# A Strassen-form matmul kernel: shared homes for mixer tiles, a seventh pair of weight tiles in Strassen's form, and another order of the weight chunks

## The chip, the cores and the metric

The kernel runs on one core of a Trainium2 chip. The metric is the device time of one execution in microseconds (us). A core has five engines with queues of their own: TensorE (PE; PEld is its weight load), VectorE (DVE), ScalarE (ACT), GpSimd (POOL) and SyncE (SP, which here only issues transfers). Each engine works through its queue in order; an instruction that waits holds all behind it.

## What is computed

One layer of a decoder for 256 positions and a width of 4096, in float32. The normalised input `u` is multiplied by `w_in` (4096 x 28672). Its columns feed two mixers, a gated linear recurrence (HGRN2, 16 heads of 128) and differential attention (8 heads of 256), and two sigmoid gates. The mixers' outputs are projected, gated, added, projected by `w_out`, added to the input and normalised. Nearly all arithmetic is matmul against weights that are read once:

```python
u = rmsnorm(h, norm_w[l])
proj = u @ w_in[l]
...
y = (jax.nn.sigmoid(gate_a) * (o_a @ w_branch_a[l])
     + jax.nn.sigmoid(gate_b) * (o_b @ w_branch_b[l]))
h = h + y @ w_out[l]
```

Each head's mixer output goes through an RMS norm of its own (segments of 128 columns for HGRN2, 256 for attention) and is multiplied by the SiLU of a gate.

## The kernel before

**Numbers in two parts.** Each float32 operand is split into a rounded part `hi` and the rest `lo`; a product is three matmuls (hi hi, hi lo, lo hi). ScalarE copies a weight chunk into `hi` (line 162), VectorE subtracts to get `lo` (line 163). A chunk is 128 partitions by 1024 columns, or 512. Rings of 5 buffers each (`whi`, `wlo`) hold the split chunks; after the mixers two more of each are added. Weights arrive in a ring of three raw tiles `w` (128 x 2048, 1 MB), loaded by SyncE's queue.

**Units and pairs.** The program is a list of units, each a product of 256 rows with 1024 columns: 16 mixer units (numbered 0 to 15; two per group of heads, four HGRN groups, then four attention groups), 8 gate units (0 to 7), 8 half-length branch units and 4 output units. A unit runs over 16 pairs of 128-row weight tiles (a pair is one raw tile). A plain pair is 2 chunks, 4 output blocks each: 2 x 4 x 3 = 24 matmuls of 512 columns. A pair in Strassen's form ("S", in Winograd's variant) has 7 products, 21 matmuls, for which VectorE first makes sums of the weight blocks in the raw tile; it gives four chunks, the third of them of 512 columns. The sums of the other operand (`sf`, by `s_form`) are made once and kept in the pool `sp`, so the number of pairs in S form is limited by SBUF. Which pairs are in S form is a table of positions: `SPLIT` for mixer units 3 to 15 and gate units 0 and 1, `SPLIT_G` for gate units 2 to 6. Mixer units 0 to 2 and gate unit 7 are plain.

**The order of the work.** `Stream.take` splits weight chunks ahead of the matmuls: with `ahead` 3 in the mixers and gate unit 0 and 5 later. `ORDER` says which of the seven products each of the four chunks feeds; `p5`, `P1`, `P6`, `P7` have PSUM banks of their own, 0 to 3 are the output blocks. A scheduler places each engine's instructions; splits and the evictions at a unit's end have a higher priority than the rest. The sums of an S pair stand in `sums`: the first at chunk 0 (line 143), with it the 512-column difference `wt` in a pool of its own (line 144), and at chunk 2 the wide difference (line 148). The third chunk is split from `wt`.

**Mixer steps.** What a mixer does beside the big product (transposes, scan, scores, values, norm, gate) are small steps in a first-in, first-out list. After each pair `step(n)` takes the next two, or one if it uses TensorE, and those with TensorE only after pairs 14, 15, 0, 1 and 2, since their PSUM banks are those of the S products. Their tiles are `big` ones (128 x 1024, 4 KB per partition) with one home per name: `z`, `q`, `g`, `v`, `s1`, `s2`, and beside these `sc` (one and a half big tiles), `kx` and `qx` (half of one each). A new tile under a name waits for the last reader of the one before. `finish` makes the squares' sums by a reduction (line 697) over squares that ScalarE wrote (lines 862 and 963), and applies norm and gate in two wide multiplies (lines 710 and 711).

## Time and profile before

| | |
|---|---|
| median of 3 runs | 2788.42 us (2786.64 to 2789.74) |
| the profiled execution | 2788.72 us, its span 2786.9 us |
| TensorE, matmuls busy | 2760.9 us, 99% |
| TensorE, weight loads busy | 2274.4 us, 82% |
| VectorE busy | 2341.9 us, 84% |
| ScalarE busy | 1616.8 us, 58% |
| transfers | 597.76 MB, 214 GB/s over the span |
| weight load of 1 MB, issue to landing | 4.8 us (median) |

Rows of a group read: line, engine, operation, out<-in, shape, count, then the busy time, the mean length of one in ns, and the idle time of the engine just ahead of them with what ended it. Rows of a timeline read: start in us, length, engine, line, operation, and in brackets the engine's idle time ahead of it and what ended that. Rows of windows read: the stretch, its length, and each engine's busy time in it.

### The profile page before, as it was taken

To read this page: it belongs to the slowest core of one execution; us is meant where nothing else is said; L and a number is where in the kernel's file an instruction comes from. 1 tells how busy PE (TensorE), PEld (TensorE's weight loads), DVE (VectorE), ACT (ScalarE), POOL (GpSimd) and SP (SyncE) were. 2 spreads that over 40 slices of the span, in tenths; PEclk is the share of its full clock that TensorE was granted. 3 is DMA by queue.
4 is the path that set the end of the run, shared out by engine and by line. 5 is a ranking of instruction groups with operands and counts; after the bars stand their busy time and mean duration, and the time that the engine had idled before them with its cause. 6 is when DMAs were issued, how large, how long until landed. Compare 5 with 4: busy or idle time off the path is not lost.

```text
span 2786.9 us, 32847 instructions
## 1 busy us (share of the span) xinstructions
PE 2760.9 (99%) x12361; PEld 2274.4 (82%) x12361; DVE 2341.9 (84%) x2689; ACT 1616.8 (58%) x1937; POOL 74.6 (3%) x124
## 2 busy tenths in 40 slices
PE   9999999999999999999999999999999999999998
PEld 7888888888888888888888887778888888888886
DVE  6784888888888888888888899999877878989997
ACT  7664656656555555665556555555655554555554
POOL 0010000000000000000000000000000000010000
PEclk9999999999999999999999999999999999999999
DMA  9555455555555555555556555555675766766665
GB/s 343 188 181 203 180 185 202 198 199 193 188 191 210 190 192 187 198 206 189 191 196 245 201 212 211 222 214 201 241 263 218 250 218 227 259 235 237 248 255 214
DMA packets 96767, 597.76 MB, mean 214 GB/s; under 512 B 11856, under 2 KB 12128, under 8 KB 31200
## 3 DMA queue, kind: packets, MB, share of 16 engines
q1 hardware_dynamic: 88272, 566.29, 55.9%
q0 software_dynamic: 8336, 29.38, 2.8%
q8 instruction: 96, 1.57, 0.2%
q14 instruction: 63, 0.52, 0.1%
HBM read 571.51 MB, written 24.12 MB: 214 GB/s over the span
## 4 chain that ended last, share of the span: by engine, by line
PE 78%; DVE 14%; DMA 4%; issue 2%; ACT 2%; POOL 0%; DVEq 0%; ACTq 0%; POOLq 0%
PE ps_w L286 75%; DVE lo L163 9%; DVE w L148 2%; DMA w<-in_w_gate 1%; ACT hi L162 1%; DMA w<-in_w_out 1%; DVE w L143 1%; DVE wt L144 1%; PE ps_q L759 1%; DMA w<-in_w_mix 0%; DMA yl<-y_dram 0%; DVE ut L369 0%; PE ps_sc L842 0%; PE ps_o L857 0%; PE ps_t L718 0%
## 5 line engine op out<-in xcount | busy, mean ns | idle before, releaser
L162 ACT ACTIVATE hi<-w 128x1024 fp32r<-128x1024 f32 (+1 forms) x1203 | 1231.5, 1053 | 1009.8 <-PE ps_w L286 497.4
L163 DVE TENSOR_TENSOR lo<-w,hi 128x1024 fp32r<-128x1024 f32 (+1 forms) x1203 | 1436.9, 1219 | 309.0 <-ACT hi L162 291.8
L286 PE MATMUL ps_w<-hi,u 128*128 128x512 f32 x4794 | 1538.8, 391 | 2.0 <-ACT hi L162 2.0
L286 PEld LDWEIGHTS ps_w<-hi,u 128*128 128x128 f32 x4794 | 900.6, 188 | 189.9 <-ACT hi L162 3.4
L286 PE MATMUL ps_w<-lo,u 128*128 128x512 f32 x2397 | 935.5, 390 | 0.9 <-DVE lo L163 0.9
L286 PEld LDWEIGHTS ps_w<-lo,u 128*128 128x128 f32 x2397 | 450.5, 188 | 99.0 <-DVE lo L163 7.1
L286 PE MATMUL ps_w<-hi,sf 128*128 128x512 f32 x1400 | 490.0, 390 | 0.8 <-ACT hi L162 0.7
L286 PEld LDWEIGHTS ps_w<-hi,sf 128*128 128x128 f32 x1400 | 262.8, 188 | 56.9 <-ACT hi L162 1.6
L286 PE MATMUL ps_w<-lo,sf 128*128 128x512 f32 x700 | 274.1, 392 | 8.1 <-DVE lo L163 7.9
L286 PE MATMUL ps_w<-hi,oh 128*128 128x512 f32 x864 | 272.4, 390 | 0.0
L286 PE MATMUL ps_w<-hi,y 128*128 128x512 f32 x784 | 250.1, 390 | 0.0
L148 DVE TENSOR_TENSOR w<-w,wt 128x1024 f32<-128x1024 f32 x175 | 213.6, 1220 | 0.3
L286 PEld LDWEIGHTS ps_w<-hi,oh 128*128 128x128 f32 x864 | 162.2, 188 | 34.3 <-DVE ut L531 1.0
L286 PEld LDWEIGHTS ps_w<-hi,y 128*128 128x128 f32 x784 | 147.2, 188 | 30.7 <-DVE ut L623 0.3
L286 PE MATMUL ps_w<-lo,oh 128*128 128x512 f32 x432 | 168.4, 390 | 0.0
L286 PEld LDWEIGHTS ps_w<-lo,sf 128*128 128x128 f32 x700 | 131.3, 188 | 41.5 <-DVE lo L163 14.7
L143 DVE TENSOR_TENSOR w<-w 128x512 f32<-128x512 f32 x175 | 120.5, 690 | 48.5 <-DMA w<-in_w_mix 27.0
L286 PE MATMUL ps_w<-lo,y 128*128 128x512 f32 x392 | 152.6, 389 | 0.0
L162 ACT ACTIVATE hi<-wt 128x512 fp32r<-128x512 f32 x175 | 109.8, 628 | 48.0 <-PE ps_w L286 32.1
L144 DVE TENSOR_TENSOR wt<-w 128x512 f32<-128x512 f32 x175 | 120.6, 689 | 2.8
L163 DVE TENSOR_TENSOR lo<-wt,hi 128x512 fp32r<-128x512 f32 x175 | 120.1, 686 | 1.8 <-ACT hi L162 1.8
L286 PEld LDWEIGHTS ps_w<-lo,oh 128*128 128x128 f32 x432 | 81.1, 188 | 16.6
(206 smaller groups left out, 1106.5 us busy)
## 6 DMA issues: line engine op xcount, KB each, us to landing
w<-in_w_mix SPq DMA_DIRECT2D x252, 1024.0 KB, 4.8
w<-in_w_gate SPq DMA_DIRECT2D x128, 1024.0 KB, 4.8
w<-in_w_branch SPq DMA_DIRECT2D x64, 1024.0 KB, 4.8
w<-in_w_out SPq DMA_DIRECT2D x64, 1024.0 KB, 5.3
gl<-g_dram SPq DMA_DIRECT2D x32, 256.0 KB, 3.7
g_dram<-ut POOLq DMA_DIRECT2D x28, 256.0 KB, 5.4
o_dram<-s POOLq DMA_DIRECT2D x8, 512.0 KB, 5.9
ol<-o_dram SPq DMA_DIRECT2D x16, 256.0 KB, 4.2
```

The source lines that it names most:

```text
L143: dve.tensor_tensor(w[:, 0:512], w[:, 0:512], w[:, 512:1024], op=ALU.add)
L144: dve.tensor_tensor(t, w[:, 0:512], w[:, 1536:2048], op=ALU.subtract)
L148: dve.tensor_tensor(b, b, t.unsqueeze(1).to_broadcast([P, 2, 512]), op=ALU.subtract)
L162: act.activation(hi[:, k : k + m], t[:, k : k + m], AF.Copy)
L163: dve.tensor_tensor(lo[:, k : k + m], t[:, k : k + m], f32(hi[:, k : k + m]), op=ALU.subtract)
L286: pe.matmul(ps[b], a, w, start=first, stop=left[b] == 0)
L759: pe.transpose(ps[:, j], r[:, j * P : (j + 1) * P], ident)
```

## The change

Five things change together.

1. **Homes.** `sc`, `kx`, `qx` and `wt` lose their own memory. Scores go into `s1` and into the first half of the old `b` tile (home `s2`), whose two halves take `kx` and `qx`; attention's exponentials take `s1` and `s2`, its transposed weights `q`; the mixer's output moves from `s2` to `z`, the gate's SiLU from `z` to `s2`.
2. **Norm.** ScalarE's squares are taken per segment with a running sum (`accum_out`), ahead of the copy, so the squares' tile and VectorE's reduction go. Norm and gate are applied in one instruction per segment, 8 of 128 columns for HGRN2 or 4 of 256 for attention, in place of two of 1024.
3. **A seventh pair.** `sp` holds 7 tiles, not 6. `SPLIT` is (4, 6, 7, 9, 10, 12, 13), was (4, 6, 8, 10, 12, 13). `SPLIT_G` keeps nine positions, with 0 and 8 out and 7 and 9 in: (2, 4, 6, 7, 9, 10, 12, 13, 14).
4. **Chunk order of an S pair.** The raw columns 1024 to 2047 (output blocks 0 and 1) come first, `p5` and `P1` second. The narrow difference is written in place over columns 1536 to 2047 once the first chunk has been split, and the wide difference follows it.
5. **`SPLIT_AHEAD`** is 4, was 3.

```diff
--- before.py
+++ after.py
@@ -35,7 +35,7 @@
 HALF = PIECE // 2
-SPLIT_AHEAD = 3
+SPLIT_AHEAD = 4
 HEAD = 4
@@ -50,8 +50,7 @@
     wlo = ctx.enter_context(tc.tile_pool(name="wlo", bufs=5))
-    wt = ctx.enter_context(tc.tile_pool(name="wt", bufs=1))
-    sp = ctx.enter_context(tc.tile_pool(name="sp", bufs=6))
+    sp = ctx.enter_context(tc.tile_pool(name="sp", bufs=7))
     gp = ctx.enter_context(tc.tile_pool(name="gp", bufs=5))
         def __init__(self):
@@ -136,16 +136,12 @@
 
-        def sums(self, i, c):
+        def sums(self, i):
             w = self.raw[i]
-            if c == 0:
-                t = self.raw[i, "T"] = wt.tile([P, 512], F32, name="wt", tag="wt")
-                dve.tensor_tensor(w[:, 0:512], w[:, 0:512], w[:, 512:1024], op=ALU.add)
-                dve.tensor_tensor(t, w[:, 0:512], w[:, 1536:2048], op=ALU.subtract)
-            if c == 2:
-                t = self.raw[i, "T"]
-                b = w[:, 512:1536].rearrange("p (a c) -> p a c", a=2)
-                dve.tensor_tensor(b, b, t.unsqueeze(1).to_broadcast([P, 2, 512]), op=ALU.subtract)
+            t2 = w[:, 1536:2048]
+            dve.tensor_tensor(t2, w[:, 0:512], t2, op=ALU.subtract)
+            b = w[:, 512:1536].rearrange("p (a c) -> p a c", a=2)
+            dve.tensor_tensor(b, b, t2.unsqueeze(1).to_broadcast([P, 2, 512]), op=ALU.subtract)
 
@@ -153,9 +149,15 @@
                 with tc.high_priority(AHEAD):
+                    o = c * HALF
                     if self.kind[i] == "S":
-                        self.sums(i, c)
-                    t = self.raw[i, "T"] if c == 2 else self.raw[i][:, (0, 1024, 0, 512)[c] :]
+                        if c == 0:
+                            w = self.raw[i]
+                            dve.tensor_tensor(w[:, 0:512], w[:, 0:512], w[:, 512:1024], op=ALU.add)
+                        if c == 2:
+                            self.sums(i)
+                        o = (1024, 0, 1536, 512)[c]
+                    t = self.raw[i][:, o:]
                     w = 512 if c == 2 else HALF
@@ -163,7 +165,6 @@
                     del self.raw[i]
-                    self.raw.pop((i, "T"), None)
                 self.split[self.done] = (hi, lo)
@@ -260,7 +261,7 @@
 
-    ORDER = (("p5", "P1"), (0, 1), ("P6",), ("P7", 2))
+    ORDER = ((0, 1), ("p5", "P1"), ("P6",), ("P7", 2))
 
@@ -435,10 +436,10 @@
 
-    SPLIT = (4, 6, 8, 10, 12, 13)
-    SPLIT_G = (0, 2, 4, 6, 8, 10, 12, 13, 14)
+    SPLIT = (4, 6, 7, 9, 10, 12, 13)
+    SPLIT_G = (2, 4, 6, 7, 9, 10, 12, 13, 14)
     us = {}
-    s_pools = [sp] * 6
+    s_pools = [sp]
 
@@ -460,7 +461,7 @@
         if n == 0:
-            s_pools[:] = [sp2] * 3
+            s_pools[:] = [sp2]
         if n in SPLIT_G and n not in SPLIT:
@@ -569,7 +570,7 @@
                 if n == 0:
-                    s_pools[:] = [sp] * 6 + [sp2]
+                    s_pools[:] = [sp]
                     s_pool.at = -1
@@ -681,34 +682,29 @@
 
-        def half(tag):
-            return tmp.tile([P, HPG, P], F32, name=tag, tag=tag)
-
         def rows(t):
...
             n = 1024 // seg
-            o, sq, g = T["o"], T["sq"], T["g"]
+            o, ss, g = T["o"], T["ss"], T["g"]
 
             def stats():
-                ss = tmp.tile([P, n], F32, name="ss", tag="ss", bufs=2)
-                dve.tensor_reduce(ss, fl(sq).rearrange("p (n c) -> p n c", c=seg), axis=AX.X, op=ALU.add)
                 act.activation(ss, ss, AF.Sqrt, scale=1.0 / seg, bias=eps)
                 dve.reciprocal(ss, ss)
-                T["ss"] = ss
 
             def gate():
-                sg = big("z")
+                sg = big("s2")
                 act.activation(fl(sg), fl(g), AF.Sigmoid)
...
             def apply():
-                o3 = fl(o).rearrange("p (n c) -> p n c", c=seg)
-                dve.tensor_tensor(o3, o3, T["ss"].unsqueeze(2).to_broadcast([P, n, seg]), op=ALU.mult)
-                dve.tensor_tensor(fl(o), fl(o), fl(T["silu"]), op=ALU.mult)
+                for i in range(n):
+                    c = slice(i * seg, (i + 1) * seg)
+                    dve.scalar_tensor_tensor(fl(o)[:, c], fl(o)[:, c], ss[:, i : i + 1], fl(T["silu"])[:, c],
+                                             op0=ALU.mult, op1=ALU.mult)
 
@@ -819,24 +815,24 @@
             def s1d():
-                km, kx, dec = T["z"], half("kx"), T["dec"]
-                dve.tensor_tensor(km, km, T["sg"], op=ALU.mult)
-                dve.tensor_tensor(kx, km[:, :, 0:P], dec[:, :, 1].to_broadcast([P, HPG, P]), op=ALU.mult)
-                T["kx"] = kx
+                dve.tensor_tensor(T["z"], T["z"], T["sg"], op=ALU.mult)
 
             def s2():
-                qm, qx, dec = T["q"], half("qx"), T["dec"]
+                qm, km, dec = T["q"], T["z"], T["dec"]
                 dve.tensor_tensor(qm, qm, T["b"], op=ALU.mult)
-                dve.tensor_tensor(qx, qm[:, :, P:S], dec[:, :, 2].to_broadcast([P, HPG, P]), op=ALU.mult)
-                T["qx"] = qx
+                x = fl(T["b"]).rearrange("p (x h c) -> p x h c", x=2, h=HPG)
+                dve.tensor_tensor(x[:, 0], km[:, :, 0:P], dec[:, :, 1].to_broadcast([P, HPG, P]), op=ALU.mult)
+                dve.tensor_tensor(x[:, 1], qm[:, :, P:S], dec[:, :, 2].to_broadcast([P, HPG, P]), op=ALU.mult)
+                T["x"] = x
 
...
                     if tb == 0:
-                        T["sc"] = tmp.tile([P, 3, HPG, P], F32, name="sc", tag="sc")
-                    sc = T["sc"][:, tb]
+                        s = fl(big("s1")).rearrange("p (t h c) -> p t h c", t=2, h=HPG)
+                        T["sc"] = s[:, 0], s[:, 1], T["x"][:, 0]
+                    sc = T["sc"][tb]
                     c = slice(tb * P, (tb + 1) * P)
-                    k, q = (T["kx"], T["qx"]) if tb == 2 else (T["z"][:, :, c], T["q"][:, :, c])
+                    k, q = (T["x"][:, 0], T["x"][:, 1]) if tb == 2 else (T["z"][:, :, c], T["q"][:, :, c])
                     ps = spare([P, HPG, P], "ps_sc")
@@ -849,17 +845,21 @@
                     if tb == 0:
-                        T["o"], T["sq"] = big("s2"), big("s1")
+                        T["o"] = big("z")
+                        T["ss"] = tmp.tile([P, 1024 // P], F32, name="ss", tag="ss", bufs=2)
                     sc, v = T["sc"], rows(T["v"])
...
                         c = slice(h * P, (h + 1) * P)
-                        pe.matmul(ps[:, h], sc[:, tb, h], v[:, tb, c], start=True, stop=(tb == 0))
+                        pe.matmul(ps[:, h], sc[tb][:, h], v[:, tb, c], start=True, stop=(tb == 0))
                         if tb:
-                            pe.matmul(ps[:, h], sc[:, 2, h], v[:, 0, c], start=False, stop=True)
+                            pe.matmul(ps[:, h], sc[2][:, h], v[:, 0, c], start=False, stop=True)
                     pf = ps.rearrange("p h c -> p (h c)")
-                    act.activation(rows(T["o"])[:, tb], pf, AF.Copy)
-                    act.activation(rows(T["sq"])[:, tb], pf, AF.Square)
+                    o = rows(T["o"])[:, tb]
+                    for h in range(HPG):
+                        i = tb * HPG + h
+                        act.activation(o[:, h * P : (h + 1) * P], ps[:, h], AF.Square, accum_out=T["ss"][:, i : i + 1])
+                    act.activation(o, pf, AF.Copy)
                 return f
@@ -910,11 +910,9 @@
                                        channel_multiplier=1, compare_op=ALU.is_ge, fill=NEG)
-                    if hh == 0:
-                        T["ee"] = tmp.tile([P, 3, HPG, P], F32, name="ee", tag="sc")
-                    ee = T["ee"].rearrange("p a h c -> p (a h c)")[:, 768 * hh : 768 * (hh + 1)]
+                    ee = fl(big(("s1", "s2")[hh]))
                     e0 = ee[:, :256].rearrange("p (i s) -> p i s", i=2)
-                    e1 = ee[:, 256:].rearrange("p (i s) -> p i s", i=2)
+                    e1 = ee[:, 256:768].rearrange("p (i s) -> p i s", i=2)
                     for qb, e in ((0, e0), (1, e1)):
@@ -944,23 +942,29 @@
                     pe.transpose(ps[:, S : S + P], e1[:, 0, P:S], ident)
-                    aT = half(("kx", "qx")[hh]).rearrange("p h c -> p (h c)")
-                    act.activation(aT[:, : 3 * P], ps[:, : 3 * P], AF.Copy)
+                    if hh == 0:
+                        T["aq"] = fl(big("q"))
+                    aT = T["aq"][:, hh * 384 : (hh + 1) * 384]
+                    act.activation(aT, ps[:, : 3 * P], AF.Copy)
                     T["aT", hh] = aT
...
                     if hh == 0:
-                        T["o"], T["sq"] = big("s2"), big("s1")
+                        T["o"] = big("z")
+                        T["ss"] = tmp.tile([P, 1024 // 256], F32, name="ss", tag="ss", bufs=2)
                     aT, v = T["aT", hh], rows(T["v"])
...
                     pe.matmul(ps[:, 1], aT[:, S : S + P], v[:, 1, c], start=False, stop=True)
-                    act.activation(rows(T["o"])[:, :, c], ps, AF.Copy)
-                    act.activation(rows(T["sq"])[:, :, c], ps, AF.Square)
+                    o = rows(T["o"])[:, :, c]
+                    for t in range(2):
+                        i = 2 * t + hh
+                        act.activation(o[:, t], ps[:, t], AF.Square, accum_out=T["ss"][:, i : i + 1])
+                    act.activation(o, ps, AF.Copy)
                 return f
```

How instructions move on VectorE. In the names `w` is the raw tile, `hi` and `lo` the split chunk. Before the change, in mixer unit 7, around the neighbouring S pairs 12 and 13 (L143 is an S pair's first sum, L144 its `wt`, L148 its wide difference); the piece begins with the wide difference of pair 12:

```order
L148 TENSOR_TENSOR w<-w,wt 128x1024
L143 TENSOR_TENSOR w<-w 128x512
L144 TENSOR_TENSOR wt<-w 128x512
L163 TENSOR_TENSOR lo<-w,hi 128x1024 x3
L163 TENSOR_TENSOR lo<-wt,hi 128x512
L148 TENSOR_TENSOR w<-w,wt 128x1024
L163 TENSOR_TENSOR lo<-w,hi 128x1024
L315 TENSOR_TENSOR ut<-ps_w,ut 128x512
```

Both narrow sums of pair 13 stand ahead of the last `lo` of pair 12, and between the wide difference of pair 13 and its last `lo` stands nothing.

With the change, in mixer unit 11, pairs 7 to 10 (L156 is an S pair's first sum, L142 the narrow difference in place, L144 the wide one, L165 `lo`); the piece begins with the narrow difference of pair 7:

```order
L142 TENSOR_TENSOR w<-w 128x512
L165 TENSOR_TENSOR lo<-w,hi 128x1024
L165 TENSOR_TENSOR lo<-w,hi 128x512
L144 TENSOR_TENSOR w<-w 128x1024
L156 TENSOR_TENSOR w<-w 128x512
L165 TENSOR_TENSOR lo<-w,hi 128x1024 x5
L142 TENSOR_TENSOR w<-w 128x512
L156 TENSOR_TENSOR w<-w 128x512
L144 TENSOR_TENSOR w<-w 128x1024
L165 TENSOR_TENSOR lo<-w,hi 128x512
L165 TENSOR_TENSOR lo<-w,hi 128x1024 x3
L142 TENSOR_TENSOR w<-w 128x512
```

The narrow difference of pair 7 has moved behind the `lo` of that pair's first chunk, the one of pair 9 (behind the run of five `lo`) behind its second; the narrow `lo` of the third chunk has moved next to the wide difference, in pair 9 behind it.

The same queue and unit, from the third chunk of pair 10 to the end of pair 13:

```order
L165 TENSOR_TENSOR lo<-w,hi 128x512
L156 TENSOR_TENSOR w<-w 128x512
L165 TENSOR_TENSOR lo<-w,hi 128x1024 x5
L142 TENSOR_TENSOR w<-w 128x512
L156 TENSOR_TENSOR w<-w 128x512
L144 TENSOR_TENSOR w<-w 128x1024
L165 TENSOR_TENSOR lo<-w,hi 128x512
L165 TENSOR_TENSOR lo<-w,hi 128x1024 x3
L142 TENSOR_TENSOR w<-w 128x512
L144 TENSOR_TENSOR w<-w 128x1024
L165 TENSOR_TENSOR lo<-w,hi 128x512
L165 TENSOR_TENSOR lo<-w,hi 128x1024 x2
```

At pair 10 the first sum of pair 12 stands ahead of the last `lo`, the first entry of the run of five; at pairs 12 and 13 nothing stands between the narrow `lo` and the last.

On TensorE, with the change, in mixer unit 5 at the end of pair 10 (hi_4108 and lo_4109 are its last chunk, hi_4118 the first chunk of the plain pair 11; ps_w_3900 is the bank of `P7`):

```order
L287 MATMUL ps_w_3891<-hi_4094,sf_2082 128x512
L287 MATMUL ps_w_3891<-lo_4095,sf_2082 128x512
L287 MATMUL ps_w_3891<-hi_4094,sf_2082 128x512
L287 MATMUL ps_w_3900<-hi_4108,sf_2082 128x512
L287 MATMUL ps_w_3704<-hi_4108,u_115 128x512
L287 MATMUL ps_w_3692<-hi_4118,u_115 128x512
L287 MATMUL ps_w_3696<-hi_4118,u_115 128x512
L287 MATMUL ps_w_3700<-hi_4118,u_115 128x512
L287 MATMUL ps_w_3900<-lo_4109,sf_2082 128x512
L287 MATMUL ps_w_3900<-hi_4108,sf_2082 128x512
L287 MATMUL ps_w_3704<-lo_4109,u_115 128x512
```

Of the last chunk of pair 10 the products with `hi` and three of pair 11's have moved ahead of the first that reads lo_4109. At the end of pair 13 it is the same with two of pair 14's.

The program has 45 matmuls of 512 columns fewer than before (11718, were 11763).

## Prediction

> **What bounds the kernel now.** I read the page first: busy shares, the chain that ended last and the costliest group.
>
> ```profile
> span 2786.9 us, 32847 instructions
> PE 2760.9 (99%) x12361; PEld 2274.4 (82%) x12361; DVE 2341.9 (84%) x2689; ACT 1616.8 (58%) x1937; POOL 74.6 (3%) x124
> ...
> PE 78%; DVE 14%; DMA 4%; issue 2%; ACT 2%; POOL 0%; DVEq 0%; ACTq 0%; POOLq 0%
> ...
> L286 PE MATMUL ps_w<-hi,u 128*128 128x512 f32 x4794 | 1538.8, 391 | 2.0 <-ACT hi L162 2.0
> ```
>
> TensorE is the bound, but VectorE stands on the last chain for 14% of the span, so there are places where TensorE is fed late. A matmul's own 391 ns is no price, since matmuls overlap. The price comes from stages, so I cut the trace by windows at the first matmul of a unit: mixer units 6 and 10, then gate units 1 to 6.
>
> ```profile
> core 0: us, PE busy (x) PEld busy (x) DVE busy (x) ACT busy (x) POOL busy (x), PEclk, DMA share, GB/s
> 542.80:629.60 86.80, 86.80 (x400) 72.00 (x399) 72.34 (x75) 50.54 (x57) 0.55 (x1) 1.00 0.54 196
> 894.60:979.70 85.10, 85.10 (x385) 70.37 (x383) 71.43 (x74) 49.47 (x58) 0.55 (x1) 1.00 0.55 197
> ...
> 1505.80:1588.80 83.00, 83.00 (x368) 68.71 (x367) 74.21 (x86) 47.73 (x54) 1.79 (x4) 1.00 0.60 226
> 1588.80:1670.60 81.80, 81.46 (x358) 66.83 (x357) 75.27 (x84) 47.38 (x55) 1.61 (x3) 1.00 0.59 218
> 1670.60:1755.20 84.60, 82.67 (x359) 66.57 (x358) 79.33 (x86) 48.61 (x56) 2.16 (x4) 1.00 0.56 211
> 1755.20:1838.50 83.30, 82.07 (x358) 66.53 (x357) 77.91 (x85) 50.35 (x58) 2.16 (x4) 1.00 0.57 214
> 1838.50:1923.40 84.90, 82.51 (x359) 66.53 (x358) 80.23 (x87) 47.85 (x55) 2.16 (x4) 1.00 0.57 212
> 1923.40:2006.40 83.00, 82.07 (x358) 66.43 (x357) 78.00 (x85) 51.01 (x58) 2.17 (x4) 1.00 0.57 214
> ```
>
> Gate unit 1 holds 6 S pairs of 21 matmuls and 10 plain ones of 24, so 366 (the row's 368 counts neighbours that overlap its ends), with no gap: 83.00 / 366 = 0.2268 us per matmul at full clock. So a plain pair takes TensorE 5.44 us, an S pair 4.76. Gate units 2 to 6 hold 9 S pairs, 357 matmuls, 80.95 us; their five rows add up to 417.6, so 12.9 us are lost there. Mixer units lose nothing that counts: 86.80 is 366 matmuls (83.0) and the mixer's own small ones. VectorE is idle 14 us of each mixer unit but only 4.7 to 6.5 of a 9-S gate unit.
>
> **The change, part by part.**
>
> *The seventh pair.* Mixer units 3 to 15 and gate units 0 and 1 turn one plain pair into S form: 15 x 3 = 45 matmuls fewer, 45 x 0.2268 = **10.2 us off TensorE**. That is 0.68 us per unit.
>
> *What VectorE pays for it.* These rows are the forms that a pair is made of.
>
> ```profile
> L163 DVE TENSOR_TENSOR lo<-w,hi 128x1024 fp32r<-128x1024 f32 x1195 | 1431.8, 1223 | 308.6 <-ACT hi L162 291.4
> L162 ACT ACTIVATE hi<-w 128x1024 fp32r<-128x1024 f32 x1195 | 1226.9, 1056 | 1008.8 <-PE ps_w L286 497.4 <-DVE w L148 341.5 <-DVE w L143 68.2
> ...
> L148 DVE TENSOR_TENSOR w<-w,wt 128x1024 f32<-128x1024 f32 x175 | 213.6, 1220 | 0.3
> ```
>
> What a row costs in a full queue is the distance of starts, and the timeline of VectorE shows it, here for mixer unit 6 while it prepares the two neighbouring S pairs 12 and 13; behind it stand TensorE's first matmul on pair 12 and its first use of the last `lo` of pair 13, and ScalarE's `hi` for that chunk.
>
> ```profile
> 604.06 1.22 DVE L148 TENSOR_TENSOR w<-w,wt 128x1024 f32<-128x1024 f32 x1
> 605.20 0.69 DVE L143 TENSOR_TENSOR w<-w 128x512 f32<-128x512 f32 x1
> 605.92 0.69 DVE L144 TENSOR_TENSOR wt<-w 128x512 f32<-128x512 f32 x1
> 606.52 1.22 DVE L163 TENSOR_TENSOR lo<-w,hi 128x1024 fp32r<-128x1024 f32 x1
> 608.66 2.60 DVE L163 TENSOR_TENSOR lo<-w,hi 128x1024 fp32r<-128x1024 f32 x2 [0.91 <-ACT hi L162]
> 611.17 0.69 DVE L163 TENSOR_TENSOR lo<-wt,hi 128x512 fp32r<-128x512 f32 x1
> 611.77 1.22 DVE L148 TENSOR_TENSOR w<-w,wt 128x1024 f32<-128x1024 f32 x1
> 614.20 1.23 DVE L163 TENSOR_TENSOR lo<-w,hi 128x1024 fp32r<-128x1024 f32 x1 [1.21 <-ACT hi L162]
> ```
>
> ```profile
> 607.32 0.39 PE L286 MATMUL ps_w<-hi,sf 128*128 128x512 f32 x1
> ...
> 615.70 0.39 PE L286 MATMUL ps_w<-lo,sf 128*128 128x512 f32 x1
> ```
>
> ```profile
> 613.11 1.06 ACT L162 ACTIVATE hi<-w 128x1024 fp32r<-128x1024 f32 x1 [2.19 <-DVE w L148]
> ```
>
> Starts stand 1.14 us apart behind a 1024-wide row (604.06 to 605.20), 0.60 behind a 512-wide one (605.92 to 606.52), 0.72 where the next reads the result (605.20 to 605.92). An S pair is four wide rows and three narrow: 4 x 1.14 + 2 x 0.60 + 0.72 = 6.48 us of VectorE, a plain one 2.28. So a unit's VectorE gains 4.2 us of work while TensorE loses 0.68.
>
> On the average this fits: 72.34 + 4.2 = 76.5 of 86.1 us. But the seven pairs no longer alternate. Positions 7 to 13 run S P S S P S S, and the group P S S costs VectorE 2.28 + 2 x 6.48 = 15.24 us against 5.44 + 2 x 4.76 = 14.96 on TensorE: **VectorE has no spare time there, and each wait of its own is TensorE's.** Five `hi`/`lo` buffers let it stand four chunks ahead, no more.
>
> How near that is shows in the rows above: the last `lo` of pair 13 ended at 614.20 + 1.23 = 615.43, TensorE read it at 615.70, a margin of 0.27 us, with a plain pair between S pairs up to there.
>
> *The chunk order.* Raw columns 1024 to 2047 go first now, which need no sum. The narrow sum that feeds the third chunk (`wt`, now in place) can no longer be made ahead: it writes over columns that the first chunk reads, so it stands behind that chunk's `lo` at pair 7 and behind the second chunk's at pairs 9 to 13 (the first two listings of the change). In the old order it lay in front, at 605.92, in time that VectorE lost to ScalarE anyway (the 0.91 us ahead of 608.66). Now up to 0.72 us enter the chain to the last `lo`, less the 0.24 us that VectorE idles inside the two-row entry (2.60 against 1.14 + 1.22): about 0.5 net. Margin 0.27 - 0.5: TensorE waits about **0.25 us at pair 7**, the first neighbour pair.
>
> From there VectorE leads. Between the wide sum's start and the last `lo` lie 614.20 - 611.77 = 2.43 us (sum, ScalarE's `hi` from 613.11, signals). The sum fills 1.14, the narrow `lo`, now behind it, 0.60; the remaining 0.69 stays empty unless the next pair's first sum stands there, which the order gives for pair 10 alone (0.09). A group P S S so takes 15.24 + 0.09 + 0.69 = 16.0 us, 1.05 more than TensorE. Two groups, up to pairs 10 and 13: 2.1. With the 0.25: 2.35 us late at the last `lo` of pair 13.
>
> TensorE does not lose all of it. Its order there (last listing of the change) puts matmuls that need only `hi`, some of the next pair's, ahead of the first that needs this `lo`: at pair 10 four more than in a plain chunk, 4 x 0.2268 = 0.9 us; at pair 13 three, 0.7. With the larger the loss is 2.35 - 0.9 = **1.45 us per unit**. Ends: nothing lost, if VectorE enters pair 6 with more lead than at 615.43; 2.35, if the early matmuls hide nothing. I take 1.45, as both its parts come from rows of the same neighbourhood. Fourteen units (mixers 3 to 15, gate 0) have five buffers: +20.3 us. Gate unit 1 has seven and idles 83.00 - 74.21 = 8.8 us on VectorE: no loss.
>
> *Gate units 2 to 6* keep nine S pairs. Position 0 moves to 7: the unit boundary with its eight narrow eviction rows is relieved of 6.48 - 2.28 = 4.2 us, while 6 to 14 now hold seven S pairs in nine. Who is late there is known:
>
> ```profile
> PEld ps_w L286 <- DVE lo L163: 12.9, 17, 1.3
> ```
>
> that is, TensorE's weight loads, from 1588 us to 2094, for VectorE's `lo`. The unit's work on VectorE is unchanged, so what can shrink is its idle time of about 5 us: six uncovered waits of 0.69 and three of 0.09 make 4.4. Saved per unit: between 0 and 1 us; I take 0.4, **-2 us** in all, ends 0 and -5.
>
> *Mixer steps.* Nearest rows to what goes and comes:
>
> ```profile
> L932 ACT ACTIVATE ee<-ee,nm 128x128 f32<-128x128 f32 x16 | 6.3, 394 | 1.4 <-DVE nm L930 1.4
> ...
> L932 ACT ACTIVATION_READ_ACCUMULATOR ee<-ee,nm 128x1 f32 x32 | 6.0, 187 | 0.0
> ...
> L697 DVE TENSOR_REDUCE ss<-s 128x4 f32<-128x1024 f32 x4 | 4.9, 1220 | 2.9 <-ACT s L963 2.9
> ...
> L927 DVE SCALAR_TENSOR_TENSOR ee<-ps_s,bias 128x128 f32<-128x128 f32 x16 | 4.1, 282 | 3.8 <-PE ps_s L923 3.7
> ```
>
> Per HGRN group VectorE loses the reduction (1.22) and turns two wide multiplies (2 x 1.22, as the wide rows above) into eight of 128 columns (8 x 0.282 = 2.26); ScalarE's two squares become eight, each with an accumulator read: 8 x (0.394 + 0.187) = 4.6 us. All this stands beside plain pairs 15 and 0 to 3, where VectorE and ScalarE fill only 2.3 of 5.4 us per pair: nothing on the path. Uncovered, the 4.6 us on ScalarE would count in full: four groups, 18 us.
>
> [...]
>
> *Sum.* -10.2 + 20.3 - 2 = **+8.1 us** on the profiled execution's 2788.72 (span 2786.9 and 1.8 around it): 2796.8. The runs' median, 2788.42, is 0.3 lower: **2796.5 us**, 0.29% slower. Ends of the sum: -15 (2773) and +22.7 (2811).
>
> **The rivals.**
>
> *VectorE keeps its lead; faster.* The mixer's P S S groups lose nothing, because the waits for ScalarE lie where VectorE would wait for a buffer: -10.2 - 2, 2776. For it: idle 14 us per unit, a margin so far never below zero. Against: 15.24 over 14.96 leaves no place for any wait. It decides as soon as the loss per unit stays under 0.68 us.
>
> *A wash.* Early matmuls hide 1.6 us instead of 0.9; loss 0.75 per unit, 10.5 us, against 12.2: 2787.
>
> *VectorE as the bound throughout.* If its 14 us of idle time were all waits that stay, each added 4.2 us would count: 14 x 4.2 - 10.2 = +49, 2837. Against it: mixer units show TensorE without gaps. [...]
>
> *Shared homes block.* A tile that waits for its home holds ScalarE's or VectorE's queue, and the `hi` behind it: the 18 us above beside the forecast, 2815. Against: each home's last reader ran at least one pair earlier in the step list.
>
> **How the numbers follow.** Forecast 0.60, VectorE keeps its lead 0.14, a wash 0.21, the two others 0.05 together. What is under 0.2%, 5.6 us, can't be told from no change here: 2782.8 to 2794.0. Slower gets the forecast, less a little of its lower end, and the last two: 0.63; same the wash and that end: 0.23; faster: 0.14. The range runs from 2783, below the wash, to 2807, past the middle between the forecast and the sum's upper end.
>
> **What would show it.** Right: mixer units longer by about 0.8 us in spite of three matmuls fewer, with waits of weight loads or matmuls for `lo` at pairs 7, 10 and 13, where there were none; VectorE's idle before the last `lo` near 0.7; gate units 2 to 6 close to 83 us with their waits moved off the unit's first pairs. Wrong: mixer units 0.7 us shorter without such waits, or gate units near 81. A wait of ScalarE on a mixer tile would speak for blocked homes.

## The result

| | before | changed |
|---|---|---|
| median | 2787.79 us (4 runs, 2786.64 to 2789.74) | 2806.41 us (4 runs, 2804.05 to 2812.46) |
| the profiled execution, its span | 2788.72, 2786.9 | 2804.05, 2802.3 |

The changed kernel is slower: ratio 1.0069, interval 1.0057 to 1.0081, or +18.6 us between the medians. The forecast was 2796.5, +0.29%: the right side, but less than half of the loss. The two profiled executions lie 15.3 us apart, because that of the change is the fastest of its four (2.4 under its median) and that of before lies 0.9 above its median. What follows accounts for these 15.3.

The head of the page and the chain that ended last, changed kernel:

```profile
span 2802.3 us, 32888 instructions
PE 2766.6 (99%) x12316; PEld 2262.2 (81%) x12316; DVE 2382.6 (85%) x2788; ACT 1640.2 (59%) x2047; POOL 78.7 (3%) x124
...
PE 71%; DVE 16%; DMA 6%; ACT 4%; issue 2%; POOL 0%; ACTq 0%; DVEq 0%; POOLq 0%
```

45 matmuls fewer (12361 to 12316), and yet a longer span; TensorE's share of the last chain went from 78 to 71%. VectorE has 41 us more work, and its busy share went from 84 to 85%, which doesn't say where the time went. The windows by stage do. Before, mixer units 0 to 2, unit 1 of them, and units 3 to 15:

```profile
6.90:280.40 273.50, 273.01 (x1235) 226.67 (x1236) 187.61 (x250) 166.55 (x222) 8.44 (x4) 0.99 0.62 228
97.60:189.80 92.20, 91.93 (x428) 76.64 (x426) 84.79 (x123) 61.15 (x80) 7.06 (x2) 1.00 0.50 183
280.40:1421.50 1141.10, 1140.82 (x5192) 943.53 (x5191) 966.80 (x1091) 687.69 (x828) 13.39 (x19) 1.00 0.54 195
```

Changed: units 0 to 2, unit 1 of them, units 3 to 15, of these 6 and 10; then gate units 0 and 1, and gate units 2 to 6 together.

```profile
6.60:285.20 278.60, 273.80 (x1236) 227.62 (x1237) 187.59 (x261) 168.22 (x237) 12.57 (x4) 0.99 0.62 224
95.80:193.00 97.20, 92.65 (x427) 77.38 (x426) 87.55 (x129) 61.97 (x81) 11.28 (x2) 0.98 0.52 184
...
285.20:1439.40 1154.20, 1146.29 (x5154) 931.43 (x5153) 1000.53 (x1173) 701.82 (x914) 13.51 (x19) 1.00 0.53 192
548.80:636.80 88.00, 87.39 (x399) 71.03 (x397) 75.01 (x87) 52.89 (x73) 0.55 (x1) 1.00 0.52 193
906.60:992.30 85.70, 85.31 (x382) 69.47 (x380) 73.05 (x80) 50.93 (x66) 0.55 (x1) 1.00 0.53 196
1439.40:1524.70 85.30, 84.80 (x374) 68.80 (x373) 73.38 (x81) 52.01 (x68) 1.20 (x3) 1.00 0.54 196
1524.70:1608.20 83.50, 82.98 (x364) 67.79 (x363) 73.46 (x82) 47.19 (x54) 1.51 (x3) 1.00 0.63 230
...
1608.20:2022.40 414.20, 408.57 (x1786) 333.87 (x1786) 394.99 (x428) 247.95 (x281) 10.79 (x20) 1.00 0.57 214
```

Units 3 to 15 took 13.1 us more (1154.2 against 1141.1), the plain units 0 to 2 took 5.1 more, gate unit 0 some 1.0 and gate unit 1 0.6 (before: 84.3 and 83.0); gate units 2 to 6 took 3.4 less (414.2 against 417.6). All that follows moved by -0.6.

**The waits that the prediction named.** The waits of TensorE and its weight loads on `hi` and `lo` over units 3 to 15, first before, then changed. A row is: who waits, on what, us in total, times, the longest.

```profile
PEld ps_w L286 <- DVE lo L163: 4.7, 13, 0.4
```

```profile
PEld ps_w L287 <- ACT hi L164: 18.5, 40, 0.7
PEld ps_w L287 <- DVE lo L165: 14.2, 25, 0.9
PE ps_w L287 <- ACT hi L164: 3.0, 14, 0.2
PE ps_w L287 <- DVE lo L165: 2.7, 8, 0.5
```

Before there was one short wait per unit; now there are several, at three places. Between starts of matmuls the trace shows the new ones at pairs 7, 10 and 13, and nearly nowhere else: about 0.5, 0.5 and 0.8 us in the mean of the fourteen units with five buffers (mixer units 3 to 15 and gate unit 0); the short wait of before, 0.2 us at pair 14, is gone. VectorE at pair 13 of mixer unit 6:

```profile
619.26 0.68 DVE L142 TENSOR_TENSOR w<-w 128x512 f32<-128x512 f32 x1
619.98 1.23 DVE L144 TENSOR_TENSOR w<-w 128x1024 f32<-128x1024 f32 x1
621.12 0.69 DVE L165 TENSOR_TENSOR lo<-w,hi 128x512 fp32r<-128x512 f32 x1
622.57 2.36 DVE L165 TENSOR_TENSOR lo<-w,hi 128x1024 fp32r<-128x1024 f32 x2 [0.76 <-ACT hi L164]
```

The idle time ahead of the last `lo` is 0.76 us, where 0.69 was forecast. What was not forecast is that more than half of the waiting is for `hi` (21.5 of 38.4 us). ScalarE and TensorE's weight loads at the same place:

```profile
621.48 2.00 ACT L164 ACTIVATE hi<-w 128x1024 fp32r<-128x1024 f32 x2
```

```profile
623.53 0.30 PEld L287 LDWEIGHTS ps_w<-hi,u 128*128 128x128 f32 x2 [0.65 <-ACT hi L164]
```

Those `hi,u` loads belong to pair 14, whose matmuls stand ahead of the first that needs the late `lo`. They were to cover 0.7 to 0.9 us. But ScalarE copies pair 14's `hi` behind that of pair 13's last chunk, which itself waits for the wide sum (ended 621.21): pair 14's was ready at 623.48, and the cover waited as well.

**A wait that nobody named.** In mixer unit 1, which is plain before and after, TensorE stood still for 4.55 us. TensorE, changed kernel:

```profile
191.28 2.08 PE L854 MATMUL ps_o<-v,s 128*128 128x128 f32 x8 [4.55 <-POOL s L841]
193.01 0.77 PE L287 MATMUL ps_w<-hi,u 128*128 128x512 f32 x1
```

It waited for GpSimd's causal mask on the scores (`score`, an `affine_select`). GpSimd, changed and then before, and TensorE before:

```profile
180.53 11.28 POOL L841 TENSOR_SCALAR_AFFINE_SELECT s<-s 128x512 f32<-128x512 f32 x2 [168.87 <-DVE u L391]
```

```profile
182.38 7.06 POOL L845 TENSOR_SCALAR_AFFINE_SELECT sc<-sc 128x512 f32<-128x512 f32 x2 [170.27 <-ACT sc L843]
```

```profile
188.85 1.16 PE L857 MATMUL ps_o<-v,sc 128*128 128x128 f32 x8 [0.27 <-POOL sc L845]
```

Before, TensorE came 0.27 us too early for it; in the change the two masks take 4.2 us more. And when TensorE resumed, it ran at half its clock (PEclk, the third column from the right, in three short windows):

```profile
191.20:193.00 1.80, 1.72 (x8) 1.72 (x9) 0.00 (x0) 0.00 (x0) 0.61 (x2) 0.50 0.63 264
193.00:196.40 3.40, 3.40 (x10) 2.72 (x10) 0.90 (x2) 2.15 (x10) 0.00 (x0) 0.50 0.00 0
196.40:200.00 3.60, 3.60 (x17) 2.96 (x17) 1.29 (x2) 2.10 (x3) 0.00 (x0) 1.00 0.02 5
```

So unit 1 took some 5 us more (97.2 after 92.2), and unit 2, which begins at 193.0, 1.5 us more.

### The profile page after: what moved, and what is told of

Read it like the earlier page. It is cut to its first block, busy times and chain, and to the rows that moved or that the text cites. A ratio compares the mean times of both kernels' runs of the same rounds, so it can differ in the third digit from the quotient of the medians.

```text
span 2802.3 us, 32888 instructions
## 1 busy us (share of the span) xinstructions
PE 2766.6 (99%) x12316; PEld 2262.2 (81%) x12316; DVE 2382.6 (85%) x2788; ACT 1640.2 (59%) x2047; POOL 78.7 (3%) x124
## 4 chain that ended last, share of the span: by engine, by line
PE 71%; DVE 16%; DMA 6%; ACT 4%; issue 2%; POOL 0%; ACTq 0%; DVEq 0%; POOLq 0%
PE ps_w L287 68%; DVE lo L165 10%; ACT hi L164 4%; DMA w<-in_w_gate 3%; DVE w L144 2%; DMA w<-in_w_mix 2%; DVE w L156 1%; DVE w L142 1%; DMA w<-in_w_out 1%; DMA yl<-y_dram 0%; PE ps_q L755 0%; POOL s L841 0%; PE ps_s L921 0%; PE ps_o L854 0%; PE ps_sc L838 0%
## 5 line engine op out<-in xcount | busy, mean ns | idle before, releaser
L164 ACT ACTIVATE hi<-w 128x1024 fp32r<-128x1024 f32 (+1 forms) x1408 | 1351.6, 994 | 1047.5 <-PE ps_w L287 448.0
L165 DVE TENSOR_TENSOR lo<-w,hi 128x1024 fp32r<-128x1024 f32 (+1 forms) x1408 | 1568.9, 1145 | 303.5 <-ACT hi L164 297.8
L287 PE MATMUL ps_w<-hi,u 128*128 128x512 f32 x4644 | 1504.5, 392 | 6.4 <-ACT hi L164 4.3
L287 PEld LDWEIGHTS ps_w<-hi,u 128*128 128x128 f32 x4644 | 870.6, 188 | 199.1 <-ACT hi L164 17.5
L287 PE MATMUL ps_w<-lo,u 128*128 128x512 f32 x2322 | 905.5, 390 | 2.1 <-DVE lo L165 2.1
L287 PE MATMUL ps_w<-hi,sf 128*128 128x512 f32 x1520 | 533.8, 391 | 0.0
L287 PE MATMUL ps_w<-lo,sf 128*128 128x512 f32 x760 | 300.7, 396 | 9.2 <-DVE lo L165 7.2
L144 DVE TENSOR_TENSOR w<-w 128x1024 f32<-128x1024 f32 x190 | 231.9, 1221 | 2.4
L156 DVE TENSOR_TENSOR w<-w 128x512 f32<-128x512 f32 x190 | 130.4, 686 | 26.3 <-DMA w<-in_w_mix 11.5
L142 DVE TENSOR_TENSOR w<-w 128x512 f32<-128x512 f32 x190 | 130.2, 685 | 1.3
L287 PEld LDWEIGHTS ps_w<-lo,y 128*128 128x128 f32 x392 | 73.6, 188 | 15.2
```

Of the source, the lines that this page charges most:

```text
L142: dve.tensor_tensor(t2, w[:, 0:512], t2, op=ALU.subtract)
L144: dve.tensor_tensor(b, b, t2.unsqueeze(1).to_broadcast([P, 2, 512]), op=ALU.subtract)
L156: dve.tensor_tensor(w[:, 0:512], w[:, 0:512], w[:, 512:1024], op=ALU.add)
L164: act.activation(hi[:, k : k + m], t[:, k : k + m], AF.Copy)
L165: dve.tensor_tensor(lo[:, k : k + m], t[:, k : k + m], f32(hi[:, k : k + m]), op=ALU.subtract)
L287: pe.matmul(ps[b], a, w, start=first, stop=left[b] == 0)
```

## The experiments

Two theories stood. *Lead*: VectorE (with ScalarE behind it) is late at neighbouring S pairs, through the seventh pair and the chunk order together. *The mask*: the seventh pair's sums for the other operand, made in unit 1, hold GpSimd's mask back. The rivals: the shared homes, the norm or `ahead` cost the time; or one of the two parts, pair or order, costs it alone. Times of units are those of each run's profiled execution, which lies up to 5.4 us off the median of its runs; windows follow as units 0 to 2, units 3 to 15, gate units 2 to 6, unless said otherwise.

### Six pairs at the old places, everything else changed

```diff
-    SPLIT = (4, 6, 7, 9, 10, 12, 13)
-    SPLIT_G = (2, 4, 6, 7, 9, 10, 12, 13, 14)
+    SPLIT = (4, 6, 8, 10, 12, 13)
+    SPLIT_G = (0, 2, 4, 6, 8, 10, 12, 13, 14)
```

> The changed kernel with the old positions of the S pairs, 6 per mixer unit and (0, 2, 4, 6, 8, 10, 12, 13, 14) in gate units 2 to 6; homes, norm, chunk order and split-ahead 4 stay changed. If the neighbouring S pairs are what costs (my theory), mixer units 3 to 15 and gate unit 0 lose only at pair 13, at most 0.5 us each, and lie within 0.5 us of the kernel before: 2788 to 2795 us. If the shared homes or the norm's new form cost the time, it stays above 2800 us and TensorE or ScalarE waits on mixer tiles. If the 4.8 us wait for GpSimd's mask in mixer unit 1 comes from the homes it stays; if it comes from the seventh pair's sums on VectorE it goes, and 6 us with it.

2792.96 us (10 runs, 2787.47 to 2796.09), ratio 1.0019 (1.0009 to 1.0028).

```profile
6.20:278.50 272.30, 271.76 (x1237) 225.57 (x1237) 186.48 (x255) 167.78 (x236) 10.10 (x4) 1.00 0.63 230
278.50:1424.00 1145.50, 1142.52 (x5193) 943.07 (x5191) 960.39 (x1109) 692.53 (x888) 12.96 (x19) 1.00 0.54 194
1591.50:2009.70 418.20, 410.36 (x1787) 334.56 (x1785) 395.41 (x426) 248.82 (x281) 10.26 (x19) 1.00 0.58 217
```

Without the seventh pair the stall of unit 1 is gone (272.3), and two thirds of the mixers' loss; 4.4 us stay in units 3 to 15 though the S pairs stand as before. That is the new chunk order's, or the homes'.

### The old chunk order with seven pairs

`ORDER`, `sums` and the tile `wt` as before, the rest changed; for room one tile less in the pool of the extra sums.

```diff
-    ORDER = ((0, 1), ("p5", "P1"), ("P6",), ("P7", 2))
+    ORDER = (("p5", "P1"), (0, 1), ("P6",), ("P7", 2))
...
-    sp2 = ctx.enter_context(tc.tile_pool(name="sp2", bufs=3))
+    sp2 = ctx.enter_context(tc.tile_pool(name="sp2", bufs=2))
```

> The changed kernel with the old chunk order (first sum and wt ahead, wt in a tile of its own; for its room the pool sp2 has 2 tiles, not 3). Seven pairs at the new positions. If the neighbouring pairs alone cost, the losses at pairs 7, 10 and 13 stay near 1.7 us per mixer unit: 2800 to 2810 us. If the chunk order put half of them there (my step: 0.5 us at pair 7 and 0.69 of uncovered wait per pair), pair 7 loses nothing and the unit loses 0.3 to 1.0: 2792 to 2800 us. If the order is all of it, mixer units are 0.68 us shorter than before: about 2785 us.

2795.97 us (10 runs, 2789.56 to 2800.15), ratio 1.0024 (1.0015 to 1.0034).

```profile
6.20:284.00 277.80, 273.24 (x1235) 226.94 (x1236) 187.62 (x261) 168.44 (x237) 12.52 (x4) 0.99 0.62 225
284.00:1423.70 1139.70, 1136.06 (x5153) 934.27 (x5152) 998.94 (x1174) 702.91 (x918) 15.09 (x19) 1.00 0.54 195
1590.00:2010.30 420.30, 411.96 (x1787) 332.25 (x1786) 393.45 (x428) 244.18 (x281) 10.79 (x20) 1.00 0.57 211
```

Units 3 to 15 take 14.5 us less than in the change, and are even 1.4 below before. Unit 1's stall stays (277.8): it goes with the seventh pair, not with the order. In gate units 2 to 6, which have seven buffers, the old order is worse by 6.1. The units at the end took some 8 us more, which the missing tile of `sp2` may explain; that was not tried apart.

### The seven pairs spread out

`SPLIT` (3, 4, 6, 8, 10, 12, 13), `SPLIT_G` (2, 3, 4, 6, 8, 10, 12, 13, 14).

> The changed kernel with seven pairs that alternate: SPLIT (3, 4, 6, 8, 10, 12, 13), SPLIT_G (2, 3, 4, 6, 8, 10, 12, 13, 14). Everything else as changed, so the same work in all. If VectorE's run P S S P S S at pairs 7 to 13 costs the time, the losses at 7 and 10 go and the one at 13 shrinks to at most 0.5 us: mixer units 0.2 to 0.7 us shorter than before, 2785 to 2796 us, of which 6 are the wait for GpSimd's mask in unit 1 if it stays. If the seventh pair's work on VectorE costs it wherever it stands, 2803 to 2810 us.

2805.22 us (4 runs, 2802.08 to 2810.62), ratio 1.0066 (1.0051 to 1.0081). Units 3 to 15 took 1144.9, 9.3 less than in the change, so the places do count there; but gate units 2 to 6 took 424.2, 10.0 more, and unit 1's stall is the same (units 0 to 2: 279.0). A gain in one stage, and it was given back in another. Gate units 2 to 6:

```profile
1597.30:2021.50 424.20, 413.08 (x1785) 339.19 (x1786) 397.89 (x429) 249.10 (x281) 10.79 (x20) 0.98 0.57 210
```

TensorE waited 11.6 us there for VectorE's evictions, in seven pieces; the four longest, of 1.9 to 2.8 us, stand at a unit's start, and right after each the granted clock was half for 3.4 us (0.51 from 1684.2 to 1687.7, for one), an estimated 1.7 us of loss each time. Three S pairs stand in a row in these units, at 2, 3 and 4; that they make the evictions late wasn't tried apart.

### A sixth `hi` and `lo` buffer in the mixers

From chunk 700 on, in gate unit 0, the ring is five again (not shown here).

```diff
+        whi3 = ctx3.enter_context(tc.tile_pool(name="whi3", bufs=1))
+        wlo3 = ctx3.enter_context(tc.tile_pool(name="wlo3", bufs=1))
+        stream.ring = [(whi, wlo)] * 5 + [(whi3, wlo3)]
```

> The changed kernel with a sixth pair of hi and lo buffers in the mixer units (gate unit 0 and later as changed). Positions and order as changed. If the lead of four chunks is too short, a fifth adds 1.1 to 1.4 us of lead at pair 7 and takes that once from each unit's loss of 1.7: 0.4 to 0.8 us left per mixer unit, 2790 to 2797 us. If VectorE's rate in the run of neighbours decides alone (16.0 us against 14.96 per group), pair 7 loses nothing but pairs 10 and 13 still lose 1 us together: 2796 to 2801 us. If buffers do not matter, no change.

2804.32 us (4 runs, 2799.9 to 2804.83), ratio 1.0057 (1.0042 to 1.0072). Units 3 to 15 took 1149.8: only 4.4 us of the 22 that they lose against their matmuls came back. One more buffer, with the splits still called four chunks ahead, is a fifth of what is missing.

### The mask moved to VectorE

The scores are masked on their way out of PSUM, by a multiply with a triangle of ones, in place of ScalarE's copy and GpSimd's mask.

```diff
-                    act.activation(sc, ps, AF.Copy)
                     if tb < 2:
-                        pool.affine_select(sc, sc, ...)
+                        dve.tensor_tensor(sc, ps, tri.unsqueeze(1).to_broadcast([P, HPG, P]), op=ALU.mult)
+                    else:
+                        act.activation(sc, ps, AF.Copy)
```

> The changed kernel, but the causal mask of the HGRN scores is a multiply on VectorE that reads the scores from PSUM (in place of ScalarE's copy and GpSimd's mask, 8 tiles in all). Theory: in mixer unit 1 GpSimd's mask got no access while VectorE ran sums with two SBUF inputs back to back (10.7 us for a mask that takes 0.6 to 1.3 elsewhere), TensorE idled 4.8 us for it and then ran at half rate for some 3 us. If so, mixer units 1 and 2 are 5 and 1.5 us shorter and the rest is as changed: 2798 to 2801 us. If the wait has another source (the queue of steps, the homes), unit 1 keeps its 97 us: 2804 to 2808 us.

2799.33 us (4 runs, 2795.85 to 2801.68), ratio 1.0039 (1.0024 to 1.0054), 7.1 below the change. Units 0 to 2, then 3 to 15:

```profile
6.40:277.80 271.40, 271.15 (x1236) 225.57 (x1237) 188.39 (x263) 166.81 (x235) 3.05 (x2) 1.00 0.62 231
277.80:1432.40 1154.60, 1146.08 (x5155) 931.68 (x5153) 1003.41 (x1179) 699.24 (x909) 5.28 (x13) 1.00 0.53 192
```

Units 0 to 2 took 7.2 us less, units 3 to 15 stand where they stood (the profiled executions as a whole differ by 5.0). The stall was the mask's, and with it went the stretch at half clock (granted clock 1.00).

### Homes, norm and `ahead` alone

Six pairs at the old places and the old chunk order, with the shared homes, the new norm and `SPLIT_AHEAD` 4.

```diff
-    SPLIT = (4, 6, 7, 9, 10, 12, 13)
+    SPLIT = (4, 6, 8, 10, 12, 13)
...
-    ORDER = ((0, 1), ("p5", "P1"), ("P6",), ("P7", 2))
+    ORDER = (("p5", "P1"), (0, 1), ("P6",), ("P7", 2))
```

> Six pairs at the old positions and the old chunk order, as before; changed alone are the homes, the norm's form and the split-ahead of 4. If these are free, as I costed them, every mixer unit is within 0.3 us of the kernel before: 2785 to 2790 us. If the 0.34 us per mixer unit that six pairs in the new order lost came from homes or split-ahead, mixer units 3 to 15 sum to 1144 to 1146 us (before: 1141) and the time is 2790 to 2795 us.

2788.2 us (10 runs, 2786.44 to 2790.47), ratio 0.9998 (0.9988 to 1.0007). Units 3 to 15:

```profile
279.90:1420.20 1140.30, 1138.83 (x5193) 944.23 (x5191) 954.28 (x1109) 692.01 (x888) 11.58 (x19) 1.00 0.54 195
```

Free: the rival of blocked homes falls. And the 4.4 us of the first experiment (5.2 against this one) are the chunk order's.

### Two chunk orders, and the mask on VectorE

A third kind of pair: the old order, with `wt` in the mixers' own memory, for the mixers and gate unit 0; the new one from gate unit 1 on.

```diff
+    ORDERS = {"S": (("p5", "P1"), (0, 1), ("P6",), ("P7", 2)), "N": ((0, 1), ("p5", "P1"), ("P6",), ("P7", 2))}
...
-            kinds = PLAIN if m < 3 else mix(16, SPLIT)
+            kinds = PLAIN if m < 3 else mix(16, SPLIT, "S")
```

> Seven pairs at the changed positions, shared homes and norm as changed, mask on VectorE; the old chunk order (with wt in the mixers' memory) in mixer units and gate unit 0, the new order from gate unit 1 on. Theory: with five buffers the new order costs the mixers 1.1 us per unit, with seven it gains. Then mixer units 3 to 15 sum to about 1140 us (changed: 1154), unit 1 is at 92, gate units 2 to 6 sum to 414: 2783 to 2788 us, at most 0.2% faster than before. Rival, that the seventh pair costs what it saves in either order: 2788 to 2794 us.

2785.46 us (10 runs, 2783.77 to 2794.39), ratio 0.9996 (0.9987 to 1.0006).

```profile
6.70:278.10 271.40, 271.13 (x1236) 225.54 (x1237) 188.46 (x263) 166.89 (x235) 1.84 (x2) 1.00 0.62 230
278.10:1418.10 1140.00, 1136.14 (x5155) 934.28 (x5153) 1001.12 (x1180) 699.50 (x912) 6.29 (x13) 1.00 0.53 195
1585.50:2000.40 414.90, 408.66 (x1787) 333.90 (x1787) 394.98 (x428) 247.99 (x281) 10.80 (x20) 1.00 0.58 214
```

Both causes are repaired, 21 us come back, and the seventh pair has then brought nothing that can be measured: units 3 to 15 at 1140.0, where 39 matmuls fewer than before would make 1132.3.

### S pairs as neighbours from the start of a unit

As the kernel just above, with `SPLIT` (4, 5, 7, 8, 10, 11, 13), `SPLIT_G` (2, 4, 5, 7, 8, 10, 11, 13, 14).

> As the kernel with two orders, but the neighbouring S pairs stand early: SPLIT (4, 5, 7, 8, 10, 11, 13), SPLIT_G (2, 4, 5, 7, 8, 10, 11, 13, 14). If VectorE's lead at a unit's start is what the neighbours draw on, a first neighbour pair at 4 and 5 and a single one at the end lose less: mixer units 0.2 to 0.5 us shorter than with two orders, 2780 to 2786 us. If only the number of neighbour pairs counts, the same time within 2 us.

2791.47 us (10 runs, 2787.4 to 2795.78), ratio 1.0012 (1.0002 to 1.0021). Units 3 to 15, then gate units 2 to 6:

```profile
278.10:1427.50 1149.40, 1141.94 (x5155) 932.05 (x5153) 999.01 (x1180) 692.87 (x908) 5.26 (x13) 1.00 0.53 193
1594.40:2003.80 409.40, 407.35 (x1787) 334.24 (x1786) 393.78 (x427) 245.97 (x280) 10.53 (x20) 1.00 0.58 215
```

The mixers lose 9.4 us by it, where the theory had them gain; the gate units win 5.5. The same twos of S pairs with a plain pair between suit the gate units, which have seven buffers and the new order, and not the mixers, which have five and the old one.

### Six buffers with two orders

The sixth buffer once more, now in the kernel with two orders and the mask on VectorE; then with the places of the kernel just above; then, at the former places, with the splits called five chunks ahead.

> The kernel with two chunk orders and the mask on VectorE, and a sixth hi/lo buffer in the mixers (the ring is five again from chunk 700 on, in gate unit 0). Theory (what is left of the mixers' loss is VectorE's short lead at neighbouring S pairs: mixer units 3 to 15 stand at 1140.0 us against 1141.1 before, where three matmuls fewer in each would make 1132.2): a sixth chunk of lead removes half to all of it, mixer units 3 to 15 at 1132 to 1136, the time 2778 to 2782. Rival (the raw tile and the sums in it, not the buffers, set how far VectorE can be ahead; a sixth buffer gave 4.4 us of 14 with the new chunk order): mixer units 3 to 15 at 1138 to 1140, the time 2784 to 2786.

2795.25 us (9 runs, 2790.37 to 2800.71), ratio 1.0024 (1.0014 to 1.0033): a miss for both theories, since it is some 8 to 10 us *slower* than with five (7.8 by the ratios, 9.8 by the medians).

> As the kernel with two orders and six buffers, with S pairs at 4, 5, 7, 8, 10, 11, 13 in the mixers and with 2 and 14 beside them in gate units 2 to 6. With five buffers these positions took 1149.4 us in mixer units 3 to 15 and 409.4 in gate units 2 to 6. Theory (lead): the sixth buffer gives back at least half of the 9 us that the mixers lost there, 1141 to 1145, gate units unchanged at 408 to 411, the time 2782 to 2786. Rival (buffers are not the limit): mixers 1147 to 1150, the time 2788 to 2791.

2787.37 us (11 runs, 2784.17 to 2795.09), ratio 0.9998 (0.9989 to 1.0007); units 3 to 15 at 1143.9, 5.5 less than with five buffers, as the theory had it, though the time lies above its 2786; gate units 412.4, 3.0 more, though they have seven buffers in both.

> As the kernel with two orders and six buffers, with the splits called five chunks ahead of the matmuls in place of four. Theory (lead): the queues' order lets VectorE use the sixth buffer one chunk earlier, mixer units 3 to 15 at 1132 to 1135, 1 to 2 us below the one with four. Rival (the scheduler places the splits by priority, and the call's distance changes little): within 1.5 us of the one with four.

2798.49 us (5 runs, 2795.34 to 2803.92), ratio 1.0035 (1.0021 to 1.0048); units 3 to 15 at 1149.6, 1.5 less than with four ahead, which is the rival's case, but gate units 2.4 more.

At the former places VectorE waits longer for raw tiles with six buffers. From 290 to 1420 us, with five buffers, then with six:

```profile
DVE w L143 <- DMA w<-in_w_mix: 23.2, 26, 3.4
```

```profile
DVE w L146 <- DMA w<-in_w_mix: 45.2, 31, 4.4
```

With the early neighbours and six buffers it is 27.7 us. ScalarE's waits for TensorE, which frees the `hi` buffers, did not shrink: 159.7 us with five, 173.0 with six. 4.5 of the 11 us that the mixers lose fall in unit 5 alone, where TensorE waited 2.2 us for a `lo` and its granted clock was 0.56 from 500.4 to 504.3. That the ring of three raw tiles is the cause isn't shown: a fourth raw tile wasn't tried.

### Six pairs in the mixers, nine in the gate units

As the kernel with two orders and five buffers, with six S pairs in the mixers and the early neighbours in the gate units.

```diff
-    SPLIT = (4, 6, 7, 9, 10, 12, 13)
-    SPLIT_G = (2, 4, 6, 7, 9, 10, 12, 13, 14)
+    SPLIT = (4, 7, 8, 10, 11, 13)
+    SPLIT_G = (2, 4, 5, 7, 8, 10, 11, 13, 14)
```

> The kernel with two chunk orders and the mask on VectorE, with six S pairs in mixer units 3 to 15 and gate units 0 and 1, at 4, 7, 8, 10, 11, 13, and nine in gate units 2 to 6, at 2, 4, 5, 7, 8, 10, 11, 13, 14. Theory (a mixer unit with five buffers can carry six S pairs but not seven; gate units with seven buffers lose least when S pairs stand in twos with a plain pair between): mixer units 3 to 15 at 1141 to 1145 us, gate units 2 to 6 at 408 to 411 against 417.6 before, units 0 to 2 at 271 to 273, the time 2778 to 2783, 0.2 to 0.35% faster than before. Rival (neighbours at 8 and 11 cost a mixer unit as much as with seven pairs): mixer units 3 to 15 at 1148 or more, 2786 to 2790.

2781.17 us (7 runs, 2778.75 to 2782.8), **ratio 0.9969 (0.9958 to 0.998)**: faster than both kernels.

```profile
6.60:279.50 272.90, 272.68 (x1236) 226.66 (x1236) 186.63 (x257) 166.12 (x234) 3.05 (x2) 0.99 0.63 229
279.50:1419.70 1140.20, 1140.19 (x5193) 942.79 (x5192) 953.60 (x1115) 678.48 (x882) 5.26 (x13) 1.00 0.54 195
1586.90:1997.30 410.40, 407.28 (x1787) 334.50 (x1786) 392.06 (x424) 244.97 (x279) 9.90 (x19) 1.00 0.58 213
```

The gain lies in gate units 2 to 6, with seven buffers: 410.4 us, 7.2 less than before, by the new order and the places together. (In this profile the first output unit takes 6.5 us more than before: TensorE waits there for `lo` (1.9 us) and for the branch units' rows (0.8), and its granted clock was 0.51 from 2482.1 to 2485.6. What makes `lo` late there stays open.) The mixers are as fast with six pairs as with seven in the old order (1140.2 and 1140.0). The neighbours 7 and 8, 10 and 11 cost them nothing that shows; with 5 beside 4 as well they take 9.2 us more, in spite of 39 matmuls fewer.

## Why the prediction was right on the side and wrong in the size

Loss per unit is what a unit lost over the 0.68 us that its three matmuls save. The four combinations of pairs and order give the mean over mixer units 3 to 15 and gate unit 0 (five buffers each), against before:

| | old order | new order |
|---|---|---|
| six pairs | -0.06 us per unit | +0.34 |
| seven pairs | 0.57 lost, 0.68 saved: -0.11 | 1.68 lost, 0.68 saved: +1.00 |

The runs are, row by row: homes alone and six pairs; two orders and the change. Neither part alone makes the loss: 0.57 for the pair and about 0.4 for the order would be 0.97; together it is 1.68.

Two steps of the sum failed: the cover by early matmuls was taken too large (3.2 us in all), and units 0 to 2 had no term (5.0 us).

- *The seventh pair, -10.2 us.* Right: 45 matmuls fewer, and the pitch stands (gate units without a wait still take 0.2267 us a matmul).
- *Neighbouring pairs in the new order, 1.45 us per unit, +20.3.* The mechanism was right: waits at pairs 7, 10 and 13, an idle 0.61 to 0.76 us ahead of the last `lo`, the narrow sum in the chain. The size was 1.68, or +23.5. The step that failed is "TensorE does not lose all of it": the early matmuls were to hide 0.9 of 2.35, and by this sum hid about 0.67, since their own `hi` was late behind the same wide sum. That 2.35 us were late to begin with wasn't measured apart.
- *Gate unit 1 has seven buffers: no loss.* It lost 1.3 us, at pairs 10 and 12, waiting for `lo`. The kernel with the mask on VectorE runs the same program there and lost nothing (82.28 us), so it isn't a steady cost of the program there.
- *Gate units 2 to 6, -2.* -3.4; inside the range given. The waits did not leave the first pair, though: there are 0.7 to 1.5 us there in each of the five, and 0.2 to 1.9 in each at pairs 13 and 14 besides.
- *Mixer steps at nothing.* Here a term was missing, **+5.0 us** over units 0 to 2 (unit 1 +5.1, unit 2 +1.5; unit 0 -1.6, which wasn't looked into). The norm, the squares and the homes, which the step priced, are free as it said. But the seventh S pair needs sums of the other operand besides the weights', and the prediction costed only the sums in the raw tile. They stand in unit 1, on VectorE, in front of a mask on GpSimd that TensorE waits for; no term looked at units 0 to 2, which are plain in both kernels.

Sum over the profiles: -10.2 + 23.5 + 1.3 - 3.4 + 5.0 - 0.6 for the rest makes 15.6 of the 15.3. Against the forecast's +8.1 that is 5.0 for units 0 to 2, 3.2 for the mixers' term and 1.3 for gate unit 1, less 2.3 for what came out better. The measured median, 2806.4, lies just inside the range, which ends at 2807, and that is luck: the range's upper part stood for early matmuls that hide nothing, and not for a wait in units 0 to 2.

The rivals: "VectorE keeps its lead" and "a wash" fall for the change, though with the old order the wash is just what comes (0.57 lost of 0.68). "VectorE as the bound throughout" falls: it would have cost 49 us, and the profiles differ by 15.3, with the new waits at three places of a unit. "Shared homes block" falls with the experiment on the homes. Its time, 2815, is nearer to the measured 2806.4 than the forecast's 2796.5, which shows that a time alone doesn't tell one cause from another.

## What to carry to other kernels

Price an added unit of work by all that it brings, also in stages that the diff doesn't touch: the sums for the seventh pair lay in a plain unit, and their cost was another engine's. A cover counts only if what it needs itself isn't behind the same late instruction. And try order and places in each stage by itself: the new order and the early neighbours each won 5 to 6 us in the gate units, with seven buffers, and lost 14.5 and 9.4 in the mixers, with five. That the number of buffers decides this isn't shown: a sixth gave back 4.4 and 5.5 us of these, and at the changed places with the old order it cost 11.
